# A fourth weight buffer in the convolution stage of a two-layer hybrid decoder step

## The chip, the cores and the metric

The kernel runs on one core of a Trainium2 chip. The metric is device time in microseconds (us) for one execution of the whole step. The engines are named as in the profile: PE is the matrix engine (PEld its weight loads), DVE the vector engine, ACT the scalar engine, POOL the GpSimd engine, SP the sync engine, which here only issues DMA transfers.

## The reference, cut to what matters

The step runs a prompt group (512 rows) and a sample group (64 rows) through two layers with the same weights; 576 rows in all, 2048 features.

```python
hn = rms_norm(x, g)
proj = hn @ w_in                                   # layer 0: 2048 -> 8 * 1024 columns
q, k, v, z_a, gate_b, gate_c, h_in, z_b = jnp.split(proj, 8, axis=-1)
# mixer A: dilated window attention; the samples read 2048 cached keys and values
o_a = dilated_attn_sample(q, concat(k_buf, k), concat(v_buf, v), n_buf) * silu(z_a)
# mixer B: gated causal convolution of width 3
conv_out, conv_state = causal_short_conv(gate_c * h_in, conv_prev, conv_w)
o_b = gate_b * conv_out * silu(z_b)
y = x + jnp.concatenate([o_a, o_b], -1) @ w_out    # then layer 1, an S5 state space mixer
```

All is float32. The outputs are the two groups' rows, the new keys and values, the last convolution inputs and the S5 states.

## The kernel before, in words

**Matrix products.** A product of a weight matrix with the 576 rows is cut into jobs. A narrow job is 128 weight columns: 16 blocks of 128 x 128, each taken three times (high part of the weight by high part of the rows, high by low, low by high) over two halves of 288 rows, so 96 matmuls of 288 columns. Jobs 0 to 31 make q, k, v and z_a of the eight heads; jobs 32 to 63 make gate_c, h_in, gate_b and z_b, four jobs for each of eight column blocks: this is the convolution stage. Jobs 64 to 67 are the output projection of layer 0.

**The weight stream.** A job's weights come in two halves of 512 KB, tiles `w` of 128 x 1024 float32; each row of such a load is 128 floats long in memory. `load_half` issues one from SP. ACT makes the high part `wh` of a quarter job (`split_hi`, 128 x 512), DVE subtracts to get the low part `wl` (`split_lo`), and after the second `wl` of a tile its buffer is free (`give`). There are three `w` buffers in the pool `wstream` and five each of `wh` and `wl`. `loads` issues the next half while `cnt["free"]`, which starts at 3 and grows by one with each freed tile, is above the count of loads. So the load of half k waits for the second `wl` of half k - 3.

**What runs beside it.** The sample attention runs in the same stretch as the convolution jobs. Its keys and values are read from the caches in 160 tiles of 512 KB whose rows are 1024 floats, issued from POOL: `kf` (far keys, 3 buffers), which DVE multiplies with the queries `qr` and reduces to scores `fs`, and `kv` (6 buffers), which PE transposes (`tkn`) for the near keys or multiplies with the weights of the softmax (`os`) for the values. The samples go in four pairs. For each pair DVE adds a mask to the far scores (`E`), PE transposes them (`tf`), ACT copies them into the score tile `Ss` and takes the exponential, PE transposes that (`tp`), and then the value products `os` follow.

**The order.** Everything is written out by one recording pass. Each engine works through its instructions in that order, and so do the two DMA queues, SP's and POOL's. The recorder keeps a model clock per engine; side work (the attention, evacuations of finished jobs) stands in `bg` as generators, and between two eighths of a job `step` and `pump` place what the model says is ready. So a change of what the model believes to be ready can move side work by some matmuls.

**Pools.** `hook2` opens the pool `conv` for the convolution's own tiles when the set-up of the S5 matrices is done (`stage2`), and `hook3` closes it once job 63 is done. `take` puts a tile in the pool with the most room; before the change only the last stage (`open_fin`) has a second home for weights.

Of the kernel before, what the change touches and what calls it, by code (L numbers as in the profile page):

```python
# [247 lines left out]
class Pools:  # L248
# [19 lines left out]
    def close(self, cm):  # L268
        at = [i for i, (c, _) in enumerate(self.live) if c is cm][0]
        _, mine = self.live.pop(at)  # L270
        cm.__exit__(None, None, None)
        if not mine.dram and not mine.psum:
            for tag in mine.n:
                for t in self.clock.ring[(mine.name, tag)][-mine.n[tag]:]:
                    self.clock.base = max(self.clock.base, self.clock.last.get(t, 0.0))
                    self.clock.gone.add(t)
# [6 lines left out]
def hybrid_step(tc, I, O):  # L283
# [19 lines left out]
    def sub(out, a, b, eng=None):  # L303
        tt(out, a, b, ALU.subtract, eng)
# [6 lines left out]
    _, wp = pools.open("wstream")  # L311
# [88 lines left out]
    def spawn(g, prio=1):  # L400
        th = dict(g=g, w=None, prio=prio)
        if advance(th):
            bg.append(th)
            bg.sort(key=lambda x: x["prio"])

    def now():
        return clk.t["PE"]
# [55 lines left out]
    def until(f):  # L463
        while not f():
            force()
# [3 lines left out]


    jobs = []
    WS = {"p": [wp], "ahead": 4}
    wt, wh, wl = {}, {}, {}
    cnt = {"i": 0, "ld": 0, "hi": 0, "lo": 0, "free": 3, "done": 0}
    order, halves = [], []

    def add_jobs(w, cols, act_hl, evac, parts=(0, 1)):
# [19 lines left out]
    room = {"w": [3, 0], "wh": [5, 0], "wl": [5, 0]}  # L497
    home = {}

    def take(tag, shape, dtype, key):  # L500
        p = max(range(len(WS["p"])), key=lambda i: room[tag][i])
        room[tag][p] -= 1
        home[tag, key] = p
        bufs = (2 if p else 3) if tag == "w" else 6 if p else 5
        return WS["p"][p].tile(shape, dtype, name=tag, tag=tag, bufs=bufs)

    def give(tag, key):
        room[tag][home.pop((tag, key))] += 1

    def load_half():  # L510
        n, hf = halves[cnt["ld"]]
        cnt["ld"] += 1
        j = jobs[n]
        t = take("w", [P, 8, P], F32, (n, hf))
        if j["wide"]:
            SP.dma_start(out=t.rearrange("p (k a) n -> p k (a n)", k=2),
                         in_=j["w"][hf * 256:(hf + 1) * 256, j["c"]:j["c"] + 512].rearrange("(k p) n -> p k n", p=P))
        else:
            SP.dma_start(out=t, in_=j["w"][hf * 1024:(hf + 1) * 1024, j["c"]:j["c"] + P].rearrange("(k p) n -> p k n", p=P))
        wt[n, hf] = [t, 0]  # L520

    def loads(urgent):
        while cnt["ld"] < min(cnt["free"], len(halves)):
            p = max(range(len(WS["p"])), key=lambda i: room["w"][i])
            if not urgent and WS["p"][p].free("w") > max(now(), clk.t["SP"]) + EPSN:
                return
            load_half()

    def split_hi():
        n, q = order[cnt["hi"]]  # L530
        cnt["hi"] += 1
        t = wt[n, q // 2][0][:, (q % 2) * 4:(q % 2) * 4 + 4, :]
        wh[n, q] = take("wh", [P, 4, P], F32R, (n, q))
        act(wh[n, q], t)

    def split_lo():
        n, q = order[cnt["lo"]]
        cnt["lo"] += 1
        e = wt[n, q // 2]
        t = e[0][:, (q % 2) * 4:(q % 2) * 4 + 4, :]  # L540
        wl[n, q] = take("wl", [P, 4, P], F32R, (n, q))
        sub(wl[n, q], t, wh[n, q].bitcast(F32))
        e[1] += 1
        if e[1] == 2:
            del wt[n, q // 2]
            give("w", (n, q // 2))
            cnt["free"] += 1

    def pump(i):
        loads(False)  # L550
        top = min(i + WS["ahead"], len(order))
        if cnt["hi"] < top:
# [761 lines left out]
    cvs = {}  # L1314
# [267 lines left out]
    def open_sample():  # L1582
        sa["cm"], sa["p"] = pools.open("sampatt", side="right")
        sa["far"] = sa["near_done"] = sa["outs"] = sa["used"] = sa["vload"] = 0
        sa["fs"], sa["kf"], sa["kv"] = {}, {}, {}
        pp = sa["p"]
        sa["nmask"] = pp.tile([P, NP], F32, name="nmask")
        sa["newmask"] = pp.tile([P, 256], F32, name="newmask")
        sa["oS"] = qs
        POOL.dma_start(out=sa["nmask"], in_=I["c_nmask"])  # L1590
        POOL.dma_start(out=sa["newmask"], in_=I["c_newmask"])
        sa["qz"] = pp.tile([P, 2, 2, 4, 32], F32, name="qz")
        POOL.memset(sa["qz"], 0.0)
        set_qz(0)
        sa["done"] = False
        spawn(near_load(), prio=1)
        spawn(sample_near(), prio=1)
        spawn(far_load(), prio=2)
        spawn(sample_far(), prio=2)
# [334 lines left out]
    def open_B(name):  # L1934
        cm, pp = pools.open(name, side="right")
        Bt["cm"], Bt["p"] = cm, pp
        Bt["t"] = [pp.tile([P, KT, NT], F32R, name=f"{name}_hi"), pp.tile([P, KT, NT], F32R, name=f"{name}_lo")]
        Bt["got"] = set()
        Bt.pop("filled", None)
        return pp  # L1940

    def fill_o():
        ns = list(stored)
        xs = {}
        cm, pp = pools.open("fillo", side="right")

        def load(i):
            n = ns[i]
            xs[n] = pp.tile([P, NT], F32, name="ol", tag="ol", bufs=2)
            SP.dma_start(out=xs[n], in_=o_scr[n])  # L1950

        yield W("SP")
        load(0)
        load(1)
        for i, n in enumerate(ns):
            yield W("ACT", xs[n])
            x = xs.pop(n)
            yield from split_B(n, x)
            if i + 2 < len(ns):
                yield W("SP", slot=[(pp, "ol", 1)])  # L1960
                load(i + 2)
        yield W("DVE")
        close(cm)
        Bt["filled"] = True
# [55 lines left out]
    def open_fin():  # L2020
        close(Bt["cm"])
        close(EV["cm"])
        EV["cm"], EV["p"] = pools.open("evac2")
        fo["cm"], fo["p"] = pools.open("fin", side="right")
        pp = fo["p"]
        WS.update(p=[wp, pp], ahead=10)
        cnt["free"] += 2
        for tag, k in (("w", 2), ("wh", 6), ("wl", 6)):
            room[tag][1] = k
        fo["Y"] = pp.tile([P, 4, D], F32, name="Y")  # L2030
        fo["Ys"] = pp.tile([64, D], F32, name="Ys")
        fo["g"] = pp.tile([P, D], F32, name="gf")
        fo["s"] = pp.tile([P, 5, 4], F32, name="st2")
        spawn(h_again(), prio=1)

    def h_again():
        yield W("POOL")
        for i in range(5):
            for p0, p1, rows in pieces(i, h_scr[0:NP], h_scr[NP:NT]):
                yield W("POOL", flag=lambda: cnt["done"] >= 116)  # L2040
                POOL.dma_start(out=fo["Y"][p0:p1, i, :] if i < 4 else fo["Ys"][p0:p1], in_=rows)
        fo["h"] = 4
        yield W("POOL")
        POOL.dma_start(out=fo["g"], in_=I["final_norm"].unsqueeze(0).to_broadcast([P, D]))
        fo["gl"] = True
# [78 lines left out]
    def heads_done():  # L2124
        return hs["done"] == NH and "done" in st_ and cnt["done"] >= 32

    def hook2(n, q):
        if not stage2:
            if n >= 33:
                until(lambda: "done" in st_)  # L2130
            if "done" not in st_:
                return
            stage2["cm"], cvs["p"] = pools.open("conv")
        if "p" not in sa:
            if not heads_done():
                return
            close(hs["cm"])
            close(cm_rot)
            open_sample()
        if sa["done"] and "t" not in Bt:  # L2140
            close(sa["cm"])
            close(cm_pers)
            open_B("o")
            spawn(fill_o(), prio=1)

    def hook3(n, q):
        if "t" not in Bt:
            while "t" not in Bt:
                hook2(n, q)
                if "t" not in Bt:  # L2150
                    force()
        if "rstd" not in h1:
            h1["rstd"] = rstd
            spawn(x_again(), prio=1)
            spawn(m0_expand(), prio=1)
            spawn(h_turn(), prio=0)
            spawn(h_split(), prio=0)
            spawn(h_rows(), prio=0)
        if "out" not in h1 and cnt["done"] >= 64 and "filled" in Bt:
            close(stage2["cm"])  # L2160
            close(EV["cm"])
            EV["cm"], EV["p"] = pools.open("evac0b")
            h1["out"] = True
# [85 lines left out]
```

## Time and profile before

| | us |
|---|---|
| three runs | 2233.0, 2233.13, 2236.11 |
| median | 2233.13 |
| the profiled execution | 2233.51 |
| its span (first to last instruction) | 2231.7 |
| PE busy in the span | 2157.8 (97%) |
| DVE / ACT / POOL busy | 1279.8 / 687.0 / 288.1 |

The page gives busy times of each engine over the span; the views by stretch show where PE is idle. PE has little idle time in all, so each stretch must be read by itself. [...] The convolution stage with the sample attention lies between about 500 and 1060 us.

### The profile page before, as it was taken

To read this page: it belongs to the slowest core of one execution; us is meant where nothing else is said; L and a number is where in the kernel's file an instruction comes from. 1 tells how busy PE (TensorE), PEld (TensorE's weight loads), DVE (VectorE), ACT (ScalarE), POOL (GpSimd) and SP (SyncE) were. 2 spreads that over 40 slices of the span, in tenths; PEclk is the share of its full clock that TensorE was granted. 3 is DMA by queue.
4 is the path that set the end of the run, shared out by engine and by line. 5 is a ranking of instruction groups with operands and counts; after the bars stand their busy time and mean duration, and the time that the engine had idled before them with its cause. 6 is when DMAs were issued, how large, how long until landed. Compare 5 with 4: busy or idle time off the path is not lost.

```text
span 2231.7 us, 38594 instructions
## 1 busy us (share of the span) xinstructions
PE 2157.8 (97%) x15566; PEld 2010.8 (90%) x15566; DVE 1279.8 (57%) x2484; ACT 687.0 (31%) x1402; POOL 288.1 (13%) x529
## 2 busy tenths in 40 slices
PE   7999999999999899999999999999999999999997
PEld 7999999999978778879877799999999999998786
DVE  3757887875666556434333355899883534443333
ACT  4543343333222112223323332222223323333222
POOL 1013333332122122210000000000001000001000
PEclk9999999999999999999999999999999999999999
DMA  6447787777999999984655355556545633339222
GB/s 178 117 123 185 190 210 182 198 204 197 239 254 262 221 273 252 267 226 135 185 168 162 118 154 143 158 172 186 169 149 164 183 112 107 103 107 226 79 64 85
DMA packets 387018, 385.30 MB, mean 173 GB/s; under 512 B 27788, under 2 KB 314760, under 8 KB 385560
## 3 DMA queue, kind: packets, MB, share of 16 engines
q1 hardware_dynamic: 329544, 225.35, 36.9%
q0 software_dynamic: 48816, 152.24, 24.7%
q10 hardware_dynamic: 8480, 5.25, 0.8%
q8 instruction: 122, 2.00, 0.4%
q14 instruction: 56, 0.46, 0.1%
HBM read 328.01 MB, written 63.12 MB: 175 GB/s over the span
## 4 chain that ended last, share of the span: by engine, by line
PE 69%; DVE 10%; DMA 10%; issue 7%; ACT 1%; POOL 1%; SPq 0%; ACTq 0%; DVEq 0%; POOLq 0%
PE mm L219 59%; DMA w<-w_in_ab 5%; DVE m L219 4%; PE mms L219 2%; DMA kv<-cache_win_v 2%; DVE wl L219 2%; PE yps L219 2%; PE vps L219 1%; PE o L219 1%; DVE kf L219 1%; PE s L219 1%; DMA kf<-cache_win_k 1%; POOL kv L219 1%; DVE e L219 1%; PE os L219 1%
## 5 line engine op out<-in xcount | busy, mean ns | idle before, releaser
L219 DVE TENSOR_TENSOR wl<-w,wh 128x512 fp32r<-128x512 f32 x576 | 392.4, 688 | 598.8 <-ACT wh L219 576.2
L219 PE MATMUL mm<-a_hi,wh 128*128 128x288 f32 x3072 | 693.8, 308 | 7.2 <-ACT wh L219 7.2
L219 PE MATMUL mm<-a_hi,wl 128*128 128x288 f32 x3072 | 662.0, 297 | 0.0
L219 PE MATMUL mm<-a_lo,wh 128*128 128x288 f32 x3072 | 660.3, 297 | 1.0 <-DVE a_lo L219 1.0
L219 ACT ACTIVATE wh<-w 128x512 fp32r<-128x512 f32 x576 | 355.6, 626 | 629.0 <-PE mm L219 279.3
L219 PEld LDWEIGHTS mm<-a_hi,wh 128*128 128x128 f32 x3072 | 495.0, 191 | 48.6 <-issue 34.4
L219 PEld LDWEIGHTS mm<-a_lo,wh 128*128 128x128 f32 x3072 | 497.4, 190 | 1.6 <-DVE a_lo L219 1.5
L219 PEld LDWEIGHTS mm<-a_hi,wl 128*128 128x128 f32 x3072 | 497.2, 190 | 0.6 <-DVE wl L219 0.4
L219 PE MATMUL mm<-y_hi,wh 128*128 128x288 f32 x512 | 109.7, 296 | 0.0
L219 PE MATMUL mm<-y_lo,wh 128*128 128x288 f32 x512 | 109.7, 296 | 0.0
L219 PE MATMUL mm<-y_hi,wl 128*128 128x288 f32 x512 | 109.5, 296 | 0.0
L219 PE MATMUL mm<-wh,o_hi 128*128 128x512 f32 x256 | 101.8, 398 | 0.0
L219 PE MATMUL mm<-wh,a_hi 128*128 128x512 f32 x256 | 99.9, 390 | 1.6 <-DVE st L219 0.8
L219 PE MATMUL mm<-wl,o_hi 128*128 128x512 f32 x256 | 100.5, 393 | 0.0
L219 PE MATMUL mm<-wh,o_lo 128*128 128x512 f32 x256 | 100.3, 392 | 0.0
L219 PE MATMUL mm<-wh,a_lo 128*128 128x512 f32 x256 | 99.7, 389 | 0.0
L219 PE MATMUL mm<-wl,a_hi 128*128 128x512 f32 x256 | 99.6, 389 | 0.0
L219 PEld LDWEIGHTS mm<-y_hi,wh 128*128 128x128 f32 x512 | 82.5, 189 | 0.0
L219 PEld LDWEIGHTS mm<-y_lo,wh 128*128 128x128 f32 x512 | 82.5, 189 | 0.0
L219 PEld LDWEIGHTS mm<-y_hi,wl 128*128 128x128 f32 x512 | 82.5, 189 | 0.0
L219 DVE TENSOR_TENSOR m<-HV,AT 64x256 f32<-64x256 f32 (+5 forms) x120 | 68.2, 569 | 4.6 <-ACT HV L219 2.1
L219 ACT ACTIVATE S<-S,st 128x128 f32<-128x128 f32 (+3 forms) x64 | 35.2, 558 | 99.9 <-DVE st L219 99.7
(333 smaller groups left out, 2624.1 us busy)
## 6 DMA issues: line engine op xcount, KB each, us to landing
w<-w_in_ab SPq DMA_DIRECT2D x128, 512.0 KB
kv<-cache_win_v POOLq DMA_DIRECT2D x80, 512.0 KB, 10.9
w<-w_in_c SPq DMA_DIRECT2D x64, 512.0 KB
kf<-cache_win_k POOLq DMA_DIRECT2D x48, 512.0 KB, 11.9
kv<-cache_win_k POOLq DMA_DIRECT2D x32, 512.0 KB, 11.4
w<-w_out_ab SPq DMA_DIRECT2D x32, 512.0 KB
w<-w_glu SPq DMA_DIRECT2D x32, 512.0 KB
w<-w_out_c SPq DMA_DIRECT2D x32, 512.0 KB
```

The lines of the kernel that those rows point to most:

```text
L219: r = f(*a, **k)
```

## The change

The pool `conv` gets room for one more `w` tile of 512 KB, and for jobs below 64 the loader takes whichever home has more room. The count of free tiles is replaced by the room of the home in question: `loads` returns when that home has none. When the pool `conv` is closed, the second home goes with it. The last stage keeps its two extra tiles.

```diff
-    WS = {"p": [wp], "ahead": 4}
+    WS = {"p": [wp], "ahead": 4, "more": 0, "end": 0}
...
+    def spot(tag, n):
+
+        return max(range(len(WS["p"]) if n < WS["end"] else 1), key=lambda i: room[tag][i])
+
     def take(tag, shape, dtype, key):
-        p = max(range(len(WS["p"])), key=lambda i: room[tag][i])
+        p = spot(tag, key[0])
...
-        bufs = (2 if p else 3) if tag == "w" else 6 if p else 5
+        bufs = (WS["more"] if p else 3) if tag == "w" else 6 if p else 5
...
     def loads(urgent):
-        while cnt["ld"] < min(cnt["free"], len(halves)):
-            p = max(range(len(WS["p"])), key=lambda i: room["w"][i])
+        while cnt["ld"] < len(halves):
+            p = spot("w", halves[cnt["ld"]][0])
+            if room["w"][p] == 0:
+                return
...
-        WS.update(p=[wp, pp], ahead=10)
-        cnt["free"] += 2
+        WS.update(p=[wp, pp], ahead=10, more=2, end=len(jobs))
...
             stage2["cm"], cvs["p"] = pools.open("conv")
+            WS.update(p=[wp, cvs["p"]], more=1, end=64)
+            room["w"][1] = 1
...
+            WS.update(p=[wp], more=0, end=0)
             close(stage2["cm"])
```

On SP, at the loads of halves 67 to 72 (jobs 33 to 36), the rows before are these; a name's number is the tile's, and the waits are semaphores by their engine or DMA lane.

```order
L219 DMA w_6264<-w_in_ab 128x8x128 [waits DMAHW2_49,DVE_49]
L219 DMA w_6344<-w_in_ab 128x8x128 [waits DMAHW3_49,DVE_49]
L219 DMA w_6443<-w_in_ab 128x8x128 [waits DMAHW4_49,DVE_49]
L219 DMA w_6539<-w_in_ab 128x8x128 [waits DMAHW5_49,DVE_49]
L219 DMA w_6599<-w_in_ab 128x8x128 [waits DMAHW6_49,DVE_49]
L219 DMA w_6711<-w_in_ab 128x8x128 [waits DMAHW7_49,DVE_49]
```

Each load waits for DVE, which frees its buffer. Now the same place on SP reads as follows.

```order
L219 DMA w_6264<-w_in_ab 128x8x128 [waits DMAHW2_49,DVE_49]
L219 DMA w_6344<-w_in_ab 128x8x128 [waits DMAHW3_49,DVE_49]
L219 DMA w_6443<-w_in_ab 128x8x128 [waits DMAHW4_49,DVE_49]
L219 DMA w_6520<-w_in_ab 128x8x128 [waits DMASW4_49,DMASW3_49,DMASW5_49,DMASW2_49,DMASW6_49,DMASW1_49,DMASW7_49,DMASW0_49,PE_49]
L219 DMA w_6541<-w_in_ab 128x8x128 [waits DMAHW5_49,DVE_49]
L219 DMA w_6601<-w_in_ab 128x8x128 [waits DMAHW6_49,DVE_49]
L219 DMA w_6713<-w_in_ab 128x8x128 [waits DMAHW7_49,DVE_49]
```

The load of half 70 (`w_6520`) goes to the new buffer: it waits for no weight tile, but for the last users of that memory in the S5 set-up (PE's transposes `tx` and POOL's transfers). From half 71 on each load waits for the `wl` that the load before it waited for.

On ACT, at the exponential of the second pair of samples (`Ss,sst`), around jobs 45 and 46, the rows before:

```order
L219 ACTIVATE wh<-w 128x512 x2
L219 ACTIVATE Ss<-tf 128x384 x2
L219 ACTIVATE wh<-w 128x512
L219 ACTIVATE Ss,sst<-Ss,sst 128x1344
L219 ACTIVATE wh<-w 128x512
L219 ACTIVATE PTs<-tp 128x512 x2
L219 ACTIVATE tail<-u 128x2
```

And on ACT now, at the same place:

```order
L219 ACTIVATE Ss<-tf 128x384
L219 ACTIVATE wh<-w 128x512
L219 ACTIVATE Ss<-tf 128x384
L219 ACTIVATE wh<-w 128x512 x2
L219 ACTIVATE Ss,sst<-Ss,sst 128x1344
L219 ACTIVATE PTs<-tp 128x512 x2
L219 ACTIVATE wh<-w 128x512
```

The last `wh` ahead of the exponential is in both the first quarter of half 93, the first use of a fresh tile.

On PE, at the transposes `tf` of the same pair, in job 45, the rows before:

```order
L219 MATMUL mm<-a_hi,wl 128x288 x2
L219 MATMUL tf<-ident,E 128x128 x6
L219 MATMUL mm<-a_hi,wh 128x288 x2
L219 MATMUL mm<-a_lo,wh 128x288 x2
L219 MATMUL mm<-a_hi,wl 128x288 x2
```

And on PE now:

```order
L219 MATMUL mm<-a_hi,wl 128x288 x2
L219 MATMUL tf<-ident,E 128x128 x3
L219 MATMUL mm<-a_hi,wh 128x288 x2
L219 MATMUL mm<-a_lo,wh 128x288 x2
L219 MATMUL mm<-a_hi,wl 128x288 x2
```

The two threes of `tf` now stand apart, the first 36 matmuls earlier in the stream of the jobs than before and the second 12. All the attention's steps on PE up to job 44 keep their place between the matmuls; from there to job 55 they move by 12 to 36 matmuls either way; after that they stand where they stood.

## Rows read from the trace of the kernel before

**Rows 1.** The page: DMA queues as packets, MB, share of 16 engines.

```profile
q1 hardware_dynamic: 329544, 225.35, 36.9%
q0 software_dynamic: 48816, 152.24, 24.7%
```

**Rows 2.** Windows: length, busy PE, PEld, DVE, ACT, POOL, PEclk, DMA share, GB/s.

```profile
600.00:650.00 50.00, 46.63 (x340) 41.58 (x339) 40.94 (x54) 12.67 (x24) 11.96 (x23) 0.97 0.89 210
...
700.00:750.00 50.00, 40.67 (x427) 38.55 (x426) 32.48 (x45) 12.89 (x23) 7.26 (x14) 0.95 0.93 224
750.00:800.00 50.00, 49.71 (x362) 40.81 (x361) 25.15 (x31) 7.51 (x17) 14.71 (x28) 0.98 0.98 249
800.00:850.00 50.00, 45.13 (x396) 41.39 (x397) 32.47 (x52) 12.19 (x25) 11.04 (x27) 0.93 0.92 256
850.00:900.00 50.00, 47.97 (x400) 41.81 (x400) 29.90 (x40) 11.18 (x19) 10.42 (x20) 0.97 1.07 255
```

**Rows 3.** Waits of PE, 500 to 1075 us: total us, times, longest us.

```profile
PE tp L219 <- ACT Ss L219: 9.0, 2, 7.0
PE mm L219 <- ACT wh L219: 4.0, 2, 3.7
PE tf L219 <- DVE E L219: 3.4, 1, 3.4
PE sps L219 <- DVE KT L219: 1.8, 1, 1.8
PE to L219 <- DVE Ss L219: 1.1, 1, 1.1
```

**Rows 4.** Waits of DVE, ACT and SP's queue, same stretch, the row that matters of each.

```profile
DVE wl L219 <- ACT wh L219: 143.1, 56, 9.3
...
ACT wh L219 <- DMA w<-w_in_ab: 112.3, 24, 10.7
...
SPq L219 <- DVE wl L219: 341.5, 58, 12.8
```

**Rows 5.** Chain of waits in order of time, 540 to 1000 us: start, length, what.

```profile
543.59 6.40 PE mm L219 x48
...
573.31 23.39 DMA w<-w_in_ab
...
774.95 34.86 DMA w<-w_in_ab
```

**Rows 6.** Timeline of ACT, from 735 to 815 us: start, length, operation, idle before.

```profile
745.47 0.63 ACT L219 ACTIVATE wh<-w 128x512 fp32r<-128x512 f32 x1 [10.72 <-DMA w<-w_in_ab]
746.01 1.40 ACT L219 ACTIVATE Ss<-Ss,sst 128x1344 f32<-128x1344 f32 x1
...
799.37 1.15 ACT L219 ACTIVATE wh<-w 128x512 fp32r<-128x512 f32 x2 [9.35 <-DMA w<-w_in_ab]
809.92 1.15 ACT L219 ACTIVATE wh<-w 128x512 fp32r<-128x512 f32 x2 [9.39 <-DMA w<-w_in_ab]
```

**Rows 7.** Timeline of PE, 739 to 749 us.

```profile
747.55 1.75 PE L219 MATMUL tp<-ident,Ss 128*128 128x128 f32 x7 [7.00 <-ACT Ss L219]
```

**Rows 8.** Timeline of SP's queue: loads of halves 69, 70, 92 and 93.

```profile
515.88 0.37 SPq L219 DMA_DIRECT2D w<-w_in_ab  x1
...
525.95 0.37 SPq L219 DMA_DIRECT2D w<-w_in_ab  x1
...
708.32 0.37 SPq L219 DMA_DIRECT2D w<-w_in_ab  x1
...
719.05 0.37 SPq L219 DMA_DIRECT2D w<-w_in_ab  x1
```

**Rows 9.** Tile `tx`: times, duration ns min/median/max, first and last start.

```profile
L219 PE MATMUL tx<-ident,cn x8: 270/272/273, 404.3 to 452.2; 128*128 128x128 f32 x8
```

**Rows 10.** Windows again: two short stretches around the stalls.

```profile
745.00:755.00 10.00, 7.45 (x42) 6.41 (x43) 7.60 (x17) 5.31 (x11) 1.02 (x2) 0.66 0.61 144
...
775.00:810.00 35.00, 31.57 (x232) 27.92 (x230) 12.74 (x14) 3.08 (x6) 6.93 (x13) 1.00 1.06 315
```

More of the change, by code (lines that the diff above doesn't have):

```diff
@@ L471, in hybrid_step @@
     jobs = []
-    WS = {"p": [wp], "ahead": 4}
+    WS = {"p": [wp], "ahead": 4, "more": 0, "end": 0}
     wt, wh, wl = {}, {}, {}
-    cnt = {"i": 0, "ld": 0, "hi": 0, "lo": 0, "free": 3, "done": 0}
+    cnt = {"i": 0, "ld": 0, "hi": 0, "lo": 0, "done": 0}
     order, halves = [], []
@@ L546, in split_lo @@
             give("w", (n, q // 2))
-            cnt["free"] += 1
     def pump(i):
```

## The prediction

> **What bounds the kernel now.** I read the stretches first. PE is busy for 97% of the span, so what the change can bring is PE's idle time in its own stage, and the time PE spends at the lower clock there. Between 600 and 900 us PE is idle for 3.37, 9.33, 0.29, 4.87 and 2.03 us of five windows of 50 us, 19.9 us together [rows 2]. In the same windows the granted clock is 0.97, 0.95, 0.98, 0.93 and 0.97. [...] The stage loses about 30 us of the profiled 2233.5.
>
> Next, who ends PE's waits. Only 4.0 us are matmuls that wait for a weight part themselves; the rest are steps of the sample attention that wait for ACT or DVE: `tp` 9.0, `tf` 3.4, `sps` 1.8, `to` 1.1 [rows 3]. But ACT and DVE are in order, and the longest of their waits is the weight stream: DVE stands 143.1 us for `wh`, ACT 112.3 us in 24 waits for a `w` tile to land [rows 4]. The stall of 7.00 us shows how the one becomes the other: `tp` starts at 747.55 after the exponential, which started at 746.01, right behind a `wh` that had waited 10.72 us for its tile [rows 6, 7]. So a late tile stops PE in two ways: its matmuls run dry, or attention steps are stuck behind the waiting `wh` or `wl`.
>
> Then why tiles are late. SP's queue waits 341.5 us for `wl` to free a buffer [rows 4], so a load starts only when a tile is used up; and after the issue it takes 23.39 or 34.86 us to land [rows 5]. PE uses a tile in 6.40 us of matmuls (48 of them) [rows 5], plus what attention steps stand between; three buffers are a lead of some 20 to 25 us, too little against 34.86. The DMA engines are full in that time: share 1.06 between 775 and 810 us [rows 10].
>
> **The change part by part.** It removes no work and adds no bytes. Load k waits for the tile k - 4 instead of k - 3.
>
> The first load into the new buffer. It stands on SP right behind the load of 515.88 us and no longer waits for a `wl` until 525.95 [rows 8]. It waits for PE's `tx`, whose last starts at 452.2 [rows 9], and for POOL transfers of the same set-up. If these are over by 516, it goes out some 9.7 us earlier; were they late, everything behind it on SP would be late too, and PE would reach jobs 35 and 36 without weights. I take the first. From there on every load goes out one tile earlier: half 93, for which ACT waited until 745.47, at 708.32 instead of 719.05 [rows 6, 8].
>
> What a tile of lead is worth. While the engines are full, tiles land 10.55 us apart (799.37 to 809.92 [rows 6]). Each tile therefore comes some 7 to 10 us earlier relative to its use, as far as the lead isn't eaten, and the longest single wait is 10.72. Term by term, with the clock loss of the window in which each stands:
>
> - `tf`, 3.4, and the clock of its window 600 to 650, 0.03 x 50 = 1.5: gone, 4.9. DVE reached `E` late because `wl` held it.
> - `sps`, 1.8: gone, for the same reason.
> - `tp` at 747.55, 7.0, and the clock of the two windows around it, (0.05 + 0.02) x 50 = 3.5: gone, 10.5. The order moves here: in both programs the exponential stands behind the first `wh` of half 93, and that is the tile which now goes out 10.7 us earlier.
> - matmuls without weights and `to` behind them, 4.0 + 1.1, and the clock of 800 to 850, 3.5: not gone, and 3 us more. After the 7 us stall, POOL had no free `kv` buffer, the DMA share fell to 0.61 (745 to 755 us [rows 10]) and the weight stream caught up almost alone, at 144 GB/s, so up to 1.0 MB or two tiles in 7 us. Without the stall this pause shrinks. The weights then enter the full stretch of 775 to 810 with four buffers and up to two tiles less caught up, instead of three: one short at worst. That is 10.55 - 6.40 = 4.2 us more waiting; none at best. I take 3, nearer the worst because the tiles ahead of it are used sooner too.
> - the second `tp`, 9.0 - 7.0 = 2.0, and the clock of 850 to 900, 1.5: half, 1.8. The row does not tell how far the lead has been rebuilt by then.
>
> Sum: 4.9 + 1.8 + 10.5 - 3.0 + 1.8 = 16.0 us off. Bounds: 30 if every loss goes; and nothing, or a few us the other way, if the pauses are all the stream had. Between them stands a limit of the DMA engines: taking 1.06 as full, the windows of rows 2 leave (0.17 + 0.13 + 0.08 + 0.14) / 1.06 x 50 = 24.5 us idle, and the same bytes have to pass before PE can be past its place at 900 us. More than about 24 us can't come from this stretch, and all of it only if the engines never pause.
>
> [...]
>
> Edits that cost nothing. `spot` and the room count run while the program is written. In the last stage nothing moves: it gets its two tiles as before. Behind job 64 SP's loads of the output projection and of `ol` change places by one or two; I cost that at nothing: each is late by one load at most, and the tiles ahead of it are the cover; if that is gone it is 512 KB at the 255 GB/s of a full window [rows 2], some 2 us. Attention steps that move by 12 to 36 matmuls are on PE anyway.
>
> The profiled execution took 2233.51 us, 0.4 over the median of the runs, 2233.13. 2233.5 - 16.0 = 2217.5, which I forecast for the median too.
>
> **The rivals.**
>
> All of it comes back. Lead is what was missing, and the pauses don't matter: every wait in rows 3 goes with its clock, and only the DMA limit is left, 24.5 of 30 us. For it: the longest single wait is 10.72, about one tile's landing. Against it: it needs the engines full without a pause for 300 us. 2233.5 - 24.5 = 2209.
>
> It is given back. The engines are the bound, PE's stalls were the pauses in which the weights caught up, and a stall removed early is paid later: for it, the shares near 1.06 in rows 2 and 10. The first two terms stay (their window had the share at 0.89), 6.7 us, the third goes into the fourth: with 3 to 4 us more waiting there, 2230.
>
> Slower: the attention's transposes come too early. The first three `tf` of the second pair now stand 36 matmuls, 36 / 48 x 6.40 = 4.8 us, earlier in PE's order, though the far keys that they need come through the same full DMA engines. If the keys don't come sooner, PE stands there for 4.8 us with the matmuls behind it, drops to the lower clock (3.5 us, as after the 7 us stall) and no weight wait is shortened behind it; it decides only if the given-back case holds as well. Against it: DVE was the late one there, held by `wl`, and that is what the lead relieves. 2233.5 + 8.3 = 2242.
>
> That the buffer isn't used can't be: SP's order shows the load ahead of the `wl`.
>
> **How the numbers follow.** The forecast, 2217.5, own range 2211 to 2225: 50%. All back, 2209: 20%. Given back, 2230: 21%. Slower, 2242: 9%. What a measurement of this kernel can tell is 0.2%, 4.5 us: faster is below 2228.7, slower above 2237.6. Faster: 0.50 + 0.20 and 0.09 of the given-back case, 0.79. Same: the remaining 0.12 of it and 0.01 of the slower case, 0.13. Slower: 0.08. For the range I leave out the top of the slower case and the lowest end of the first rival: 2206 to 2231.
>
> **What would show it.** On ACT the waits for `w<-w_in_ab` should fall from 112.3 us to below 60, and DVE's for `wh` likewise. The 7.00 us before `tp` should be gone. Matmuls should still wait for `wh` somewhere in the stretch around the third pair, 5 to 10 us; if they don't, the first rival is right. The DMA share in the windows should be nearer 1.06 and the pauses shorter. PE's idle time in the stage should be below 10 us and the sample attention should end some 15 us earlier, with all behind it moved and unchanged. I am wrong if the weight waits fall and PE instead waits for `kv` or `kf` tiles to land, or if the waits for `w` don't fall.

## The result and the profile after

| | median us | runs | range us |
|---|---|---|---|
| before | 2233.91 | 4 | 2233.0 to 2236.11 |
| after | 2219.14 | 4 | 2216.24 to 2221.32 |

The ratio is 0.9934, 95% interval 0.992 to 0.9948: 14.8 us faster; the forecast was 2217.5. The profiled execution of the changed kernel took 2219.27 us, its span is 2217.4.

The stage first. The windows of the changed kernel, in the columns of [rows 2] (length, busy PE, PEld, DVE, ACT, POOL, granted clock of PE as a share of its full speed, DMA share, GB/s):

```profile
600.00:650.00 50.00, 50.00 (x374) 44.74 (x372) 38.59 (x52) 13.47 (x25) 10.91 (x21) 1.00 0.95 227
650.00:700.00 50.00, 43.91 (x313) 37.25 (x312) 22.26 (x39) 7.93 (x16) 11.65 (x28) 0.93 1.02 294
700.00:750.00 50.00, 49.42 (x506) 45.19 (x505) 37.64 (x51) 15.59 (x29) 9.80 (x19) 1.00 0.95 227
750.00:800.00 50.00, 49.37 (x361) 42.37 (x360) 27.11 (x34) 7.69 (x13) 12.64 (x25) 1.00 1.05 289
800.00:850.00 50.00, 48.82 (x501) 45.22 (x500) 35.18 (x57) 13.15 (x26) 11.02 (x27) 1.00 1.06 268
850.00:900.00 50.00, 50.00 (x378) 43.15 (x381) 33.97 (x47) 12.79 (x24) 12.52 (x24) 1.00 1.08 287
```

Of the 19.9 us of idle time in the five windows of [rows 2], 2.4 us are left, and the clock is 1.00 in all five. One window that was undisturbed before, 650 to 700 us, has a new loss: 6.09 us idle and a clock of 0.93, which, counted as the prediction counts it, is 0.07 x 50 = 3.5 us more. Before, it read:

```profile
650.00:700.00 50.00, 49.91 (x370) 43.12 (x369) 24.77 (x42) 8.32 (x17) 12.23 (x29) 1.00 1.07 305
```

What PE waited for between 500 and 1075 us (total, times, longest), to be held against [rows 3]:

```profile
PE to L219 <- DVE Ss L219: 7.3, 2, 6.1
PE os L219 <- DMA kv<-cache_win_v: 1.8, 3, 0.7
PE sps L219 <- DVE KT L219: 0.6, 1, 0.6
```

`tp`, `tf` and the matmuls that waited for `wh` are no longer there. `to`, 1.1 us before, now has 7.3, and the waits for a value tile `kv` rose from 0.4 to 1.8 us. The row that matters of ACT, of DVE and of SP's queue, in the same stretch, against [rows 4]:

```profile
ACT wh L219 <- DMA w<-w_in_ab: 43.2, 7, 11.3
...
DVE wl L219 <- ACT wh L219: 116.6, 51, 10.3
...
SPq L219 <- DVE wl L219: 428.7, 62, 15.7
```

ACT's waits for weights fell from 112.3 to 43.2 us, but the longest is as long as before. DVE's waits for `wh` fell only from 143.1 to 116.6 us. SP's queue, now a tile ahead, waits longer for `wl` than before. On it the new buffer is seen at once: halves 69 and 70 go out as a pair, where half 70 waited until 525.95 before [rows 8]:

```profile
518.24 1.05 SPq L219 DMA_DIRECT2D w<-w_in_ab  x2
```

ACT's timeline, against [rows 6]: the exponential (738.92) no longer stands behind a late `wh`. Two tiles are late at about the same time as before, by 11.33 and 9.05 us (before 9.35 and 9.39), and this time no matmul ran dry behind them.

```profile
683.26 1.15 ACT L219 ACTIVATE wh<-w 128x512 fp32r<-128x512 f32 x2 [9.02 <-DMA w<-w_in_ab]
...
738.92 1.42 ACT L219 ACTIVATE Ss<-Ss,sst 128x1344 f32<-128x1344 f32 x1 [1.16 <-DVE sst L219]
...
794.02 1.15 ACT L219 ACTIVATE wh<-w 128x512 fp32r<-128x512 f32 x2 [11.33 <-DMA w<-w_in_ab]
804.23 1.15 ACT L219 ACTIVATE wh<-w 128x512 fp32r<-128x512 f32 x2 [9.05 <-DMA w<-w_in_ab]
```

The late tiles are halves 99 and 100 now, and were 98 and 99 before: ACT works one half further ahead of PE. Before, PE multiplied their first `wh` at once, 0.7 us after ACT had begun to make it:

```profile
800.05 0.53 PE L219 MATMUL mm<-a_hi,wh 128*128 128x288 f32 x2 [0.34 <-ACT wh L219]
...
810.60 0.85 PE L219 MATMUL mm<-a_hi,wh 128*128 128x288 f32 x2 [3.69 <-ACT wh L219]
```

Now it comes to them 7.6 and 8.6 us later than ACT:

```profile
801.58 0.43 PE L219 MATMUL mm<-a_hi,wh 128*128 128x288 f32 x2
...
812.78 0.52 PE L219 MATMUL mm<-a_hi,wh 128*128 128x288 f32 x2
```

The first of ACT's rows, at 683.26, belongs to the new stall. DVE's timeline there:

```profile
673.75 1.29 DVE L219 TENSOR_TENSOR wl<-w,wh 128x512 fp32r<-128x512 f32 x2 [2.91 <-ACT wh L219]
683.92 0.69 DVE L219 TENSOR_TENSOR wl<-w,wh 128x512 fp32r<-128x512 f32 x1 [8.88 <-ACT wh L219]
684.53 1.22 DVE L219 TENSOR_TENSOR kf<-kf,qr 128x1024 f32<-128x1024 f32 x1
...
690.55 1.22 DVE L219 TENSOR_REDUCE fs<-kf 128x8 f32<-128x1024 f32 x1
...
693.55 0.74 DVE L219 TENSOR_SCALAR Ss<-os,sst 128x512 f32<-128x512 f32 x1
```

DVE stands still for 8.88 us before the `wl` of half 87, then does three products and sums of `kf` (684.53 to 691.7, 7.2 us) that could have been done in that pause, since the last of their three `kf` tiles landed at 673.9, and only then scales the attention's output `Ss`, for which PE's `to` waits:

```profile
694.35 1.12 PE L219 MATMUL to<-ident,Ss 128*128 128x128 f32 x4 [6.09 <-DVE Ss L219]
```

In the order of the kernel before, the three `kf` products stand ahead of that `wl`. The recorder places a step when its model says that the data is there, so with a fourth buffer it believed half 87 to be there earlier, and moved this `wl` forward. That is inferred from the two orders and the recorder's rule.

### The profile page after: what moved, and what is told of

It reads as the page before. It is cut to its first block, busy times and chain, and to the rows that moved or that the text cites. A ratio compares the mean times of both kernels' runs of the same rounds, so it can differ in the third digit from the quotient of the medians.

```text
span 2217.4 us, 38597 instructions
## 1 busy us (share of the span) xinstructions
PE 2154.6 (97%) x15566; PEld 2007.7 (91%) x15566; DVE 1280.4 (58%) x2484; ACT 687.5 (31%) x1402; POOL 287.7 (13%) x529
## 2 busy tenths in 40 slices
DMA packets 387018, 385.30 MB, mean 174 GB/s; under 512 B 27788, under 2 KB 314760, under 8 KB 385560
## 3 DMA queue, kind: packets, MB, share of 16 engines
q0 software_dynamic: 48816, 152.24, 24.6%
## 4 chain that ended last, share of the span: by engine, by line
PE 78%; DMA 7%; DVE 7%; issue 5%; ACT 1%; POOL 1%; SPq 0%; ACTq 0%; DVEq 0%; POOLq 0%
PE mm L219 66%; DMA w<-w_in_ab 3%; PE mms L219 2%; PE yps L219 2%; DMA kf<-cache_win_k 2%; DVE m L219 2%; PE vps L219 1%; DVE wl L219 1%; PE tkn L219 1%; DVE kf L219 1%; PE o L219 1%; PE s L219 1%; DMA U<-u_scr 1%; DMA kv<-cache_win_v 1%; PE os L219 1%
## 6 DMA issues: line engine op xcount, KB each, us to landing
kv<-cache_win_v POOLq DMA_DIRECT2D x80, 512.0 KB, 11.2
```

## The experiments

Two theories were tested. One: the lead of the loads brings the gain, and what is left is again late tiles. The rival: the order that moved, or the DMA engines as a bound, decides. The table has all runs; "stage loss" is PE's idle time between 480 and 1080 us in the profiled execution plus, as an estimate of what the clock costs, half of its time at the granted clock of 0.50 in that stretch (before: 20.4 + 10.2 = 30.6; after: 9.7 + 3.4 = 13.1). The traces show a little less than half: before, at 0.50, pairs of matmuls of 288 columns start 0.48 us apart (620.39, 620.87, 621.35), and at 1.00 0.27 us apart (623.37, 623.64, 623.90), so some 0.45 of the time is lost. Each ratio is to the kernel before on the same chip; e1 to e4, e5 to e8 and e9 to e12 ran on three chips. Outside the stage the profiled executions differ by up to 9 us (span less stage loss, 2201 to 2210), so small differences of span can't be read as the stage's.

| run | weight / kv buffers | median us (range, runs) | ratio to before (95%) | profiled span | stage loss us |
|---|---|---|---|---|---|
| e1 order of before | 4 / 6 | 2210.81 (2210.14-2213.71, 5) | 0.9913 (0.9898-0.9929) | 2208.4 | 3.4 |
| e2 after, again | 4 / 6 | 2220.6 (2215.97-2221.12, 6) | 0.9951 (0.9936-0.9966) | 2219.3 | 12.7 |
| e3 | 4 / 5 | 2221.27 (2217.07-2225.31, 7) | 0.9958 (0.9943-0.9973) | 2221.1 | 10.9 |
| e4 | 5 / 5 | 2217.58 (2214.82-2223.09, 6) | 0.9945 (0.9928-0.9962) | 2213.4 | 4.6 |
| e5 one `wl` back | 4 / 6 | 2219.02 (2213.16-2220.8, 5) | 0.9936 (0.9923-0.9948) | 2218.4 | 9.5 |
| e6 no far keys | 3 / 6 | 2225.99 (2224.44-2228.6, 7) | 0.997 (0.9959-0.998) | 2223.9 | 16.2 |
| e7 no far keys | 4 / 6 | 2227.01 (2222.53-2230.78, 10) | 0.9974 (0.9964-0.9983) | 2226.7 | 17.7 |
| e8 half-tile loads | 3 / 6 | 2208.39 (2205.62-2210.39, 4) | 0.9889 (0.9874-0.9904) | 2208.6 | 0 |
| e9 late by 8 us | 4 / 6 | 2214.3 (2210.47-2218.05, 6) | 0.9922 (0.9907-0.9937) | 2216.3 | 11.2 |
| e10 half-tile loads | 4 / 6 | 2206.14 (2204.64-2208.91, 4) | 0.9884 (0.9865-0.9902) | 2207.1 | 0.4 |
| e11 = e5 again | 4 / 6 | 2215.08 (2213.2-2222.98, 6) | 0.9932 (0.9915-0.9949) | 2213.0 | 6.3 |
| e12 = e1 again | 4 / 6 | 2213.23 (2205.5-2219.72, 6) | 0.9918 (0.9897-0.9938) | 2203.7 | 2.2 |

### The buffer without the new order (e1, e2, e12)

The recorder keeps its rules and its model of three buffers; only the memory of each fourth tile of the stage comes from the pool `conv`. Every engine has the order of before, word for word.

```diff
+        if tag == "w" and "four" in WS and key[0] < 64:
+            WS["four"] += 1
+            if WS["four"] % 4 == 1:
+                t = cvs["p"].pool.tile(shape, dtype, name=tag, tag=tag, bufs=1)
+                clk.tile((wp.name, tag), 3, t, shape)
+                return t
```

> The kernel before with every engine's instructions in exactly the order of before; only every fourth weight tile of the stage lies in a fourth buffer, so that load k waits for the second wl of tile k - 4. Theory (the lead of the loads alone brings the gain): 2217 to 2224 us, at least 10 of the 14 us gained; ACT's waits for w fall from 112.3 to 40 to 60 us, the 7.00 us before tp are gone. Rival (the order that moved, the attention steps earlier on PE, brings it): 2229 to 2234 us, with the 7.00 us before tp still there.

> The changed kernel once more beside the others. Both theories: 2216 to 2222 us. If the idle time before the first pair's to (6.1 us) is a property of the program and not of one execution, it is there again, 5 to 7 us at 685 to 695 us; if it came from the 2.4 us by which that execution was late at 500 us, it is smaller or elsewhere.

e1 came out faster than both theories allowed: 20.4 us below before, 9.8 us below e2 on the same chip, and the ranges of the two don't touch. ACT's waits for weights are 51.7 us, as the theory had them. PE's waits of e1 between 500 and 1075 us are one row:

```profile
PE os L219 <- DMA kv<-cache_win_v: 3.4, 5, 1.1
```

DVE's timeline of e1 at the place of the new stall:

```profile
672.11 1.29 DVE L219 TENSOR_TENSOR wl<-w,wh 128x512 fp32r<-128x512 f32 x2 [1.73 <-ACT wh L219]
673.32 1.22 DVE L219 TENSOR_TENSOR kf<-kf,qr 128x1024 f32<-128x1024 f32 x1
...
680.75 0.76 DVE L219 TENSOR_TENSOR c<-mm,c 128x576 f32<-128x576 f32 x1 [0.20 <-PE mm L219]
685.62 0.69 DVE L219 TENSOR_TENSOR wl<-w,wh 128x512 fp32r<-128x512 f32 x1 [4.11 <-ACT wh L219]
686.23 0.74 DVE L219 TENSOR_SCALAR Ss<-os,sst 128x512 f32<-128x512 f32 x1
```

The tile is as late as in the changed kernel (DVE gets it at 685.62, there at 683.92), but the `kf` products are already done, and `Ss` is ready 7.3 us earlier (2.2 of them because this execution came to the stage earlier: half 69 goes out at 516.0, in the changed kernel at 518.24). e2 has the stall again, so it belongs to the program:

```profile
PE to L219 <- DVE Ss L219: 7.5, 2, 6.5
```

> The order of before with four buffers, once more beside these: 2209 to 2214 us, PE idle in the stage under 5 us and no drop of the clock in it. A time above 2216 us would say that the first run of it was a lucky one.

On another chip the same program gave 2213.2 with a wide range; the profiled execution was its fastest, 2205.5, with this left in the stretch of 500 to 1075 us:

```profile
PE tf L219 <- DVE E L219: 1.7, 1, 1.7
PE os L219 <- DMA kv<-cache_win_v: 0.5, 1, 0.5
```

By the ratios the changed order costs 0.2 to 0.4% (0.9934 and 0.9951 against 0.9913 and 0.9918), 4 to 9 us; clear of the noise is only e1 against e2, on one chip, the intervals of the others overlap. The buffer alone is worth 18 to 20 us, of which the order that the recorder makes of it takes a part back.

### One instruction put back (e5, e11)

```diff
-        if cnt["lo"] < cnt["hi"]:
+        if cnt["lo"] < cnt["hi"] and not (order[cnt["lo"]] == (43, 2) and sa["far"] < 21):
```

> The changed kernel with a single instruction moved: on DVE, the first wl of half 87 stands behind the three products and sums of kf (7.3 us of work that is ready) instead of ahead of them; all other engines have the order of the changed kernel. Theory (that wl waits 9 us for a late tile with the three kf products stuck behind it, so Ss and with it PE's to come 6.5 us late): the idle time before the first pair's to is under 1.5 us, no drop of the clock at 690 us, and the time is 2209 to 2214 us, that of the run with the order of before. Rival (the other moved steps, the transposes that stand 36 matmuls earlier on PE, cost the 9 us): 2217 to 2222 us.

> The run with the one wl moved back, once more, to see whether the idle time before tf (2.3 us at 616 us, with a drop of the clock) belongs to the program or to one execution. If to one execution: no idle time before tf, and 2212 to 2217 us. If to the program: it is there again and the time is 2218 to 2221 us. Either way the idle time before the first pair's to stays under 2 us.

PE's waits of e5, and then of e11, 500 to 1075 us:

```profile
PE os L219 <- DMA kv<-cache_win_v: 3.4, 5, 1.0
PE tf L219 <- DVE E L219: 2.3, 1, 2.3
PE to L219 <- DVE Ss L219: 1.5, 1, 1.5
```

```profile
PE to L219 <- DVE Ss L219: 2.5, 2, 2.0
PE tf L219 <- DVE E L219: 2.0, 1, 2.0
PE os L219 <- DMA kv<-cache_win_v: 1.2, 3, 0.6
```

The stall did what the theory says of it: 6.5 us before the first pair's `to` became 1.5 and 2.0, and the clock no longer fell there. The time did not follow. e5's 2219.0 lies in the rival's range and not in the theory's. e11 met neither of its two cases: `tf` waits again, and the time is 2215.1. Both runs overlap with the changed kernel, and the ratios, 0.9936 and 0.9932 against 0.9934 and 0.9951, do not tell a gain from none. In e5 `tf` (2.3 us and a drop of the clock) and the `kv` waits came in its place; e11's execution kept the gain, 6.3 us less span than e2 for 6.4 less stage loss. So the stall is explained, by one `wl` ahead of work that was ready; the distance to e1 is explained by it only in part, and e5's rival, that other moved steps cost the rest, is left standing. The wait at `tf` turned up in e5, e11 and e12 and not in after, e1 or e2, although all six have the same order up to it: it belongs to the execution and not to the order.

### A recorder that is told the truth (e9)

```diff
-            end = max(self.dma, at) + 1900
+            end = max(self.dma, at) + 1900 + self.late
...
+        clk.late = 8000.0 if 32 <= n < 64 else 0.0
```

> The changed kernel written out by a recorder that takes a weight tile of this stage to land 8 us later than its model says (nothing else changes; the loads go out as early as four buffers allow). Theory (the 9 us between the changed kernel and the run with the order of before are the recorder's belief that a tile with more lead is already there, so that it puts wl ahead of work that is ready): 2210 to 2215 us, idle time in the stage under 6 us. Rival (the order of before is just a lucky one): 2216 to 2224 us.

The time is in the theory's range, 2214.3, but the profiled execution has 3.4 us before `to` and 2.6 before `tp`, a stage loss of 11.2 where under 6 was forecast. With one flat delay the recorder makes yet another order. In it the `wl` of half 87 stands ahead of one `kf` product and sum instead of three, and DVE waits 7.36 us before it: the stall before `to` is the same one, about half as long. On the same chip e9, e11 and e12, three different orders, lie within 2 us of each other (2214.3, 2215.1, 2213.2), and the changed kernel was not run there. That the belief in early tiles is the whole cost is not shown.

### Other leads (e3, e4)

One `kv` buffer less (`bufs=5`); then also a fifth weight buffer, which goes into the memory won.

> The changed kernel with five kv buffers instead of six, as the base for the next. Theory (lead against landing time, for cache tiles as for weights): POOL's queue has one tile of lead less, PE waits for kv 8 to 20 us instead of 1.8 and the time is 2222 to 2232 us; the waits for w fall a little, below 43 us. Rival (the DMA engines are the bound, leads only say where the waiting is done): 2217 to 2222 us.

> Five weight buffers up to job 54 (the fifth in the pool of the sample attention) and five kv buffers. Against the run with four and five: theory (lead) 4 to 10 us less, since the stall before the first pair's to (6.1 us and 3.4 us of clock) has a late weight tile behind it; ACT's waits for w below 20 us. Rival (DMA bound): within 3 us of it, the waiting only moves to kv or kf.

e3 waits 6.8 us for `kv`, less than the theory gave, and its time is that of e2, as the rival had it: the `kv` waits took the place of the stall at `to`, 0.7 us here. e4's stage loses 4.6 us instead of 10.9, without `to` and without a drop of the clock, but the time is only 3.7 us less, between the two forecasts and with ranges that overlap, and ACT's waits for weights are 30.9 us, not below 20; both runs moved the order too. Inconclusive on the price, in line with the lead on the stall.

### Less traffic (e6, e7)

```diff
+                if n == 0:
+                    sa["kfc"] = pp.tile([P, 1024], F32, name="kfc")
+                    POOL.dma_start(out=sa["kfc"], in_=far_ap(ck, b, t))
...
-                POOL.dma_start(out=sa["kf"][n], in_=far_ap(ck, b, t))
...
-                mul(x, x, sa["qr"])
+                mul(x, sa["kfc"], sa["qr"])
```

One far key tile is loaded and used 48 times, so the far scores are not the reference's; its buffer is one of the three of `kf`.

> The kernel before (three weight buffers) with 47 of the 48 far key loads left out: DVE multiplies the one tile each time, so the far scores are not the reference's. Theory (tiles are late because the cache loads take the DMA engines' turns): ACT's waits for w fall from 112 us to below 50, PE's idle time in the stage to below 8 us, time 2205 to 2216 us. Rival (a load needs its 25 to 35 us whatever else moves): the waits for w stay near 100 us and the time at 2222 to 2233 us.

> The changed kernel (four weight buffers) with the same 47 far key loads left out. Theory: within 4 us of the run with three buffers, since nothing is late for the fourth to cover. Rival: 10 us or more below that run.

ACT's row of e6, and PE's, 500 to 1075 us:

```profile
ACT wh L219 <- DMA w<-w_in_ab: 14.4, 4, 5.5
```

```profile
PE os L219 <- DMA kv<-cache_win_v: 9.1, 8, 2.2
PE tf L219 <- DVE E L219: 2.7, 3, 1.8
PE sps L219 <- DVE KT L219: 0.9, 1, 0.9
```

With three buffers the waits for weights fall from 112.3 to 14.4 us: tiles are late because of the other queue's traffic. And a fourth buffer then brings nothing (2227.0 against 2226.0, with the same order on every engine). e6's time missed its forecast by 10 us, and PE is idle for 12.8 us where below 8 was forecast: with far keys at hand the recorder packs the attention into less of the stage (its last `to` runs at 923 us, before at 1010), and PE waits for `kv` instead.

### Shorter loads (e8, e10)

```diff
-            POOL.dma_start(out=x, in_=f(c, b, t))
+            for c0 in (0, 512):
+                POOL.dma_start(out=x[:, c0:c0 + 512], in_=f(c, b, t)[..., c0:c0 + 512])
```

The same for `kf`.

> The kernel before with three weight buffers, each cache tile read by two loads of half the columns, so that POOL's queue has rows of 2 KB instead of 4 KB; the same bytes, 160 loads more on POOL. Theory (the two queues take turns packet by packet): SP's queue gets nearly twice the share in a full stretch, some 45 to 55 GB/s instead of 30, ACT's waits for w fall from 112 to below 70 us, and the time is 2214 to 2228 us if kv does not become late. Rival (the share goes by bytes or by the loads in flight): the waits stay near 112 us and the time at 2229 to 2238 us.

> The changed kernel (four buffers, its own order) with cache tiles read in rows of 2 KB, two loads each. Theory (an order that counts on early tiles costs only where tiles are late, and with the shorter rows they are not): 2206 to 2212 us, PE idle in the stage under 3 us, no gain over three buffers with the shorter rows. Rival (the order itself costs the 9 us, on PE, whenever tiles land): 2214 to 2220 us.

These are the fastest kernels of the study, 23.9 and 27.3 us below before; by the ratios, 0.9889 and 0.9884 against 0.9934 and 0.9951, they are 10 to 15 us below the changed kernel, though on other chips. e10, window and PE's only wait:

```profile
650.00:700.00 50.00, 50.00 (x402) 43.75 (x401) 25.64 (x46) 10.16 (x20) 24.56 (x51) 1.00 1.08 300
```

```profile
PE os L219 <- DMA kv<-cache_win_v: 0.4, 1, 0.4
```

But the mechanism that I had written down is not what happened. The DMA view (packets, MB, share of 16 engines) of a full stretch, 652 to 662 us, of before, of the changed kernel and of e8:

```profile
q0 software_dynamic: 859, 3.14, 87.4%
q1 hardware_dynamic: 858, 0.43, 15.5%
```

```profile
q0 software_dynamic: 894, 3.25, 88.2%
q1 hardware_dynamic: 892, 0.45, 15.9%
```

```profile
q0 software_dynamic: 732, 2.44, 89.2%
q1 hardware_dynamic: 746, 0.38, 16.3%
```

Before and after, POOL's queue q0 and SP's queue q1 moved nearly the same number of packets in such a stretch, 859 to 858 and 894 to 892. By the rows above a packet of q0 had 3.7 and 3.6 KB in the mean, one of q1 0.5 KB, so the weights got 0.43 MB in 10 us before, 43 GB/s of 357. It is the same with four loads in flight: between 788 and 794 us of the changed kernel, with halves 99 to 102 issued (102 at 787.4 us) and none landed (ACT waits for half 99 until 794.02), the counts are 389 to 389. In this stretch of e8 the counts are still nearly one for one (732 to 746), and the weights get 0.38 MB. Elsewhere they get more than before: between 566 and 578 us 0.49 MB (965 packets to 827), before 0.37 MB (721 to 721). So their rate did not double, and it rose by a third at most in these two. On the page of e8, POOL's queue over the whole span:

```profile
q0 software_dynamic: 51376, 152.25, 24.1%
```

That is 2560 packets more than in [rows 1], 16 for each of the 160 added loads, and they are short: the pages count 30349 packets under 512 B, before 27788. One packet for each row of 2 KB would have made some 20,000 more (160 tiles of 128 rows). The longer packets did not get shorter: those of 2 to 8 KB are 70800 on both pages (388121 - 317321 in e8, 385560 - 314760 before). SP's share did not double, and ACT still waits 57.6 us for weights in e8. What ended PE's waits there, shorter loads that land sooner (median 7.4 us from issue to landing for a `kv` half of values between 560 and 960 us, 11.7 for a whole one before), 268 GB/s instead of 251 in that stretch, or the order that the recorder made of 160 more loads, was not separated, and stays open. What e10 does show: with the shorter loads the fourth buffer adds nothing that can be told (0.9884 against 0.9889, overlapping). It is no test of the changed kernel's order: PE and ACT have the same order in e8 and e10, and DVE's differs in ten places, so the steps that moved in the changed kernel did not move here.

## Why the prediction came out right, and where it did not

The time was right within 2 us, and so was the size of the stage's loss: 14 us were to remain of 30, and 13.1 did. The 30 are 19.9 us of idle time and the deficits of the mean clock, 0.20 x 50 = 10 us [rows 2]. The clock terms thus take PE to lose half of its time at the lower level; no run shows that, and the matmuls of before show some 0.45 at 0.50 (0.48 us for a pair against 0.27). By that the clock terms in the sum, 1.5, 3.5 and half of 1.5, would be some 0.6 us smaller. The places were right in the first half and wrong in the second, and the errors cancelled. A little of the time is chance too: the changed kernel's profiled execution came to the stage 2.4 us later (half 69 goes out at 518.24, before at 515.88), with the same program up to there and a clock of 0.97 against 1.00 in its first 100 us. So the stage gave 17.5 us by its loss, where the span shows 14.3.

- The first load into the new buffer: as taken. It goes out behind its neighbour at 518.24.
- `tf` 4.9, `sps` 1.8, `tp` 10.5: gone but for 0.6 at `sps`. The mechanism holds: the exponential no longer waits behind a `wh`. In e1, with the order of before, all three are gone too, so it is the lead that did it. For `tf` the profile of after was a fortunate one: 1.7 to 2.3 us are back in e5, e11 and e12.
- Matmuls without weights and `to` behind them, "not gone, and 3 us more": this step failed. 11.6 us were to be there and 1.2 are (`to`, 808.7 us; the clock stays at 1.00). The first half of the argument is in the profile: the tiles are late by 11.33 and 9.05 us, before by 9.35 and 9.39, and the pause in which the weights caught up is gone (745 to 755 us, DMA share 1.12 where [rows 10] has 0.61). But it cost PE nothing: in this trace the `wh` made at 794.02 and 804.23 are multiplied only at 801.6 and 812.8. With the fourth buffer ACT waits for a tile that PE needs only 7.6 and 8.6 us later; before it was 0.7. A wait of ACT for a tile is not yet a wait of PE, and I had set one for the other.
- By the sign that the prediction set, no wait of matmuls for `wh` around the third pair, "all of it comes back" should have been right. It was not for this kernel, because of the loss that the next lines name. Another sign failed too: DVE's waits for `wh` were to fall as ACT's did, to below 60 us, and went from 143.1 to 116.6.
- The second `tp`, half to remain (1.7): none did.
- Not forecast: `to` of the first pair, 6.1 us and 3.5 of the clock, and `kv`, 1.8. I had looked for a cost of the moved order on PE, the transposes that stand 36 matmuls earlier (the rival "slower"). What the profile shows of it lay on DVE, where one `wl` moved ahead of three `kf` products. The rival's kind was right, its engine and its size were not.
- The terms count the lead alone and no larger share of the DMA engines for the weights. The traces agree in full stretches: SP's queue moved 858 packets to POOL's 859 before and 892 to 894 after, and with four loads in flight 389 to 389.
- The limit of 24.5 us from the DMA shares did not hold. With the loads of the changed kernel and the order of before, 3.4 (e1) and 2.2 us (e12) are left of 30.6, and in e10 0.4. A share near 1.06 is no fixed rate: 1.07 went with 255 GB/s in [rows 2], and 1.08 with 287 in the changed kernel's window of 850 to 900.

So the likeliest case was named, but the truth is nearer to two rivals at once: nearly all of the loss comes back (e1, e12), and the new order takes a part of it again.

## What to carry to other kernels

When an engine's order comes from a model, a new buffer changes two things: when data can arrive, and what the model believes has arrived; measure the buffer under the old order before judging it. A step that waits for a transfer should not stand ahead of work that is ready, on an engine that keeps its program's order as DVE did here (8.88 us idle before a `wl`, with three `kf` products behind it whose tiles had landed by 673.9): look for an idle gap that is followed at once by work that needed nothing from the gap's end. (Here PE's 6.1 and 6.5 us of idle time went when one step was put back, but a shorter time of the whole kernel was not shown for it.) And count a late tile only from the point where the last engine in the chain runs out of it.

## What was not expected of the hardware

Two loads of half the columns did not halve the length of the packets of POOL's queue: 51376 packets in e8 against 48816 before for the same 152 MB, 16 more per added load, and 70800 packets of 2 to 8 KB on both pages. And from 652 to 662 us, with the two queues at 103 and 104% of the 16 engines' time, they moved nearly the same number of packets, 859 to 858 before and 894 to 892 after, so that SP's queue, with 0.5 KB a packet, got 0.43 of 3.57 and 0.45 of 3.70 MB beside 3.7 and 3.6 KB a packet on POOL's; with four loads in flight it was 389 to 389.
